# Latent attention scores: three products of 97 and 96 rows, or two full passes and one that two key tiles share

## The chip, the cores and the metric

The kernel runs as one program on one core of a Trainium2 chip. The metric is device time in microseconds (us) from the first to the last instruction of one execution; the time before is 2669.7 us, the median of 3 runs (2669.53 to 2672.55).

## The reference

One encoder layer is applied to two groups of tokens, 2048 of them ("sample", group 0) and 512 ("prompt", group 1), with shared weights and a model width of 1024. Every token is normalised, shifted and scaled, and projected; branch A is windowed attention, branch B is latent attention over all tokens of the group, and both are gated, merged and projected again. The change is in branch B's scores. It has 8 heads; a query and a key have 64 channels of their own (`nope`) and 32 rotary ones, and all heads share the rotary key:

```
q = concatenate([q_nope, q_rope]) * scale          # 96 channels
k = concatenate([k_nope, broadcast(k_rope)])       # 96 channels
s = einsum("bqhd,bkhd->bhqk", q_blk, k)
p = softmax(s);  o = einsum("bhqk,bkhd->bqhd", p, v)
```

## The kernel before, in words

Everything is computed to nearly float32 by splitting each operand into a high part, which the matmul takes in one pass, and a low part, the rest. A product is then high x high, low x high and high x low: three matmuls into one PSUM bank. Three stages follow one another. The first (lines 199 to 624) projects the tokens in five chunks of 512 (four of group 0, one of group 1) and writes queries, keys and values to DRAM. The second (lines 641 to 857) is latent attention. The third does the rest.

In the second stage a work item is one head and one chunk of 512 queries (`items`, line 772): per head four chunks of group 0 with 2048 keys each, and the one of group 1 with 512 keys. An item is cut into units of two key tiles of 128 keys, 8 units for group 0 and 2 for group 1: 34 units a head, 272 in all. The order of the engines' work in a unit is written out by hand (`SLOTS`, line 837, under a manual schedule):

- `load`: Q and, with a new head, K and V are fetched on the SP queue, in order (`q_load` 667, `load_k` 656, `load_v` 659, and `k_tile` 646, which fetches what all heads share once for each of the two K buffers).
- `s` (`s_mm`, 713): scores, transposed, keys x queries, two key tiles into two banks of one tile of PSUM, of which there are two. Each key tile takes three matmuls, over 97, 96 and 96 rows. Row 96 of K is all ones and row 96 of Q is minus the maximum of the query, so the scores come out with the maximum taken off.
- `row` (`row_mm`, 693): TensorE transposes an item's negated maxima into PSUM; ACT copies them (`row_copy`), to Q itself in the first items, later to DRAM, from where SP loads them into Q (`row_load`).
- `v` (`v_mm`, 752): two units later, the output: two matmuls of 128 x 128 weights with the exponentials' high part, two of 128 x 64 weights with the low part.
- `mp` and `red` (`mp_mm` 675, `mp_red` 684): ahead of an item, its maxima: the high x high product of 128 queries with 1024 keys into the only PSUM tile for it, and DVE's maximum over it. In the first two items this was done in the first stage.
- `exp`, `lo`, `sum`: ACT takes the exponential twice, once to the high type (`ph`) and once to float32 (`pf`); POOL subtracts them (`pl`); DVE adds `pf` to a running sum (line 748; at an item's first unit line 742, which adds two tiles of SBUF).
- `h`: from unit 220 on, the third stage's first activations are fetched, and from unit 230 split on ACT and DVE (line 638), with one weight tile after them (line 123).

Other matmuls that the prediction reads: lines 100 to 102 (`mm3`, the three products of a projection), line 561 (small float32 products at the start, whose 2-column weights stand in four column groups of the array), line 573 after them, and line 878 (the same kind in the third stage, among projections).

Of the kernel before, what the change touches and what calls it, by code (L numbers as in the profile page):

```python
# [10 lines left out]
F32R = mybir.dt.float32r  # L11
# [7 lines left out]
P = 128  # L19
D = 1024  # L20
KD = D // P
T = 512
# [11 lines left out]
def f(ap):  # L34
    return ap.bitcast(F32)
# [3 lines left out]
def encoder(ctx: ExitStack, tc: tile.TileContext, x_prompt, x_sample, c_prompt, c_sample, b_ada, g_norm, g_q,  # L39
            w_uq, g_kv, w_ukv, sink, g_final, t_mod, t_gate, t_col, t_a, t_b, t_oa, t_ob, t_out, rope_c, rope_s, bias, sel, y_prompt, y_sample):  # L40
    nc = tc.nc
# [36 lines left out]
    qn_d = [dram.tile([HB * 64, 2, T], F32, name=f"qn_d{c}") for c in range(NC)]  # L78
    qr_d = [dram.tile([HB * 32, 2, T], F32, name=f"qr_d{c}") for c in range(NC)]
    k_d = [dram.tile([HB, 64, 2, n * T], F32, name=f"k_d{n}") for n in (NS, 1)]  # L80
    kr_d = [dram.tile([32, 2, n * T], F32, name=f"kr_d{n}") for n in (NS, 1)]
# [8 lines left out]
    rw_d = [dram.tile([HB, 4, P], F32, name=f"rw_d{c}") for c in range(NC)]  # L90
    gate_d = dram.tile([2, D], F32, name="gate_d")
    ones_d = dram.tile([P, 1024], F32, name="ones_d")
# [115 lines left out]
    with psum("ps1a", 4) as pps["a"], psum("ps1t", 1) as pps["t"], psum("ps1c", 1) as pps["c"], \  # L208
# [307 lines left out]
        with pool("p0", "right") as p0:  # L516
# [36 lines left out]
            for q in range(4):  # L553
                pm = px(("t2", "t3")[q % 2], f"pm{q}")
                for k in range(0, KD, 2):
                    wa = p0.tile([P, 2, 2, 256], F32, name=f"wa{q}_{k}", tag="wa", bufs=WB)
                    nc.sync.dma_start(wa.rearrange("p i s n -> p (i s n)"), t_mod[q, k // 2])
                    for i in range(2):
                        for n in range(2):
                            r = 32 * (2 * i + n)  # L560
                            nc.tensor.matmul(pm[r:r + 2, 0:256], sc[:, k + i, :], wa[:, i, n, :], start=(k == 0),
                                             stop=(k == KD - 2))
                if q < 2:
                    pre.append(wload(p1a, f"a0_{2 * q}", r_loads(t_a, 512, 2 * q, 2), NR))
                for i in range(4):
                    r = 32 * i
# [8 lines left out]
                ks = slice(2 * q, 2 * q + 2)  # L575
# [65 lines left out]
    with psum("ps2s", 2) as pss, psum("ps2v", 1) as ps2v, psum("ps2", 1) as ps2, pool("p2k") as pk, pool("p2q") as pq, pool("p2a") as p2a, \  # L641
            pool("p2") as p2:
        NK = {0: 4 * NS, 1: 4}
        KT, VT = {0: [], 1: []}, {0: [], 1: []}

        def k_tile(g, i, tp):
            nk = NK[g]
            KT[g].append(tp.tile([97, 2, nk * P], F32R, name=f"K{g}_{i}"))
            nc.sync.dma_start(f(KT[g][i][96:97, 0, :]),
                              ones_d[0:nk // 8 or 1, 0:min(nk * P, 1024)].rearrange("(o a) b -> o (a b)", o=1))  # L650
            nc.sync.dma_start(f(KT[g][i][64:96]), kr_d[g])

        def v_tile(g, i, tp):
            VT[g].append(tp.tile([P, NK[g], P], F32R, name=f"V{g}_{i}"))

        def load_k(g, h):
            nc.sync.dma_start(f(KT[g][h % 2][0:64]), k_d[g][h])

        def load_v(g, h):
            nc.sync.dma_start(f(VT[g][h % 2]), v_d[g][h])  # L660
# [5 lines left out]

        def q_load(it):
            nm = it.nm
            it.Q = pq.tile([97, 2, T], F32R, name=f"Q{nm}", tag="Q", bufs=4)
            nc.sync.dma_start(f(it.Q[0:64]), qn_d[it.c][it.h * 64:(it.h + 1) * 64])  # L670
            nc.sync.dma_start(f(it.Q[64:96]), qr_d[it.c][it.h * 32:(it.h + 1) * 32])
            it.mx = pq.tile([P, 4, 2], F32, name=f"mx{nm}", tag="mx", bufs=5)
            it.ng = pq.tile([P, 4], F32, name=f"ng{nm}", tag="ng", bufs=5)

# [25 lines left out]

        def row_copy(it):
            if it in items[:ND]:
                nc.scalar.copy(it.Q[96:97, 0, :], it.rp[0:1, :])
                return
            rw = pq.tile([4, P], F32R, name=f"rw{it.nm}", tag="rw", bufs=2)
            nc.scalar.copy(rw, it.rp[0:4, 0:P])
            nc.sync.dma_start(rw_d[it.c][it.h], f(rw))
            row_load(it)

        def row_load(it):  # L710
            nc.sync.dma_start(f(it.Q[96:97, 0, :]), rw_d[it.c][it.h].rearrange("(o a) b -> o (a b)", o=1))

        def s_mm(it, p):
            K, Q, nm = KT[it.g][it.h % 2], it.Q, it.nm
            ps = pss.tile([P, 2, T], F32, name=f"s{nm}_{p}", tag="s")
            for j in range(2):
                ks = slice((2 * p + j) * P, (2 * p + j + 1) * P)
                nc.tensor.matmul(ps[:, j, :], K[0:97, 0, ks], Q[0:97, 0, :], start=True, stop=False)  # L718
                nc.tensor.matmul(ps[:, j, :], K[0:96, 1, ks], Q[0:96, 0, :], start=False, stop=False)  # L719
                nc.tensor.matmul(ps[:, j, :], K[0:96, 0, ks], Q[0:96, 1, :], start=False, stop=True)  # L720
            it.s = ps

        def s_exp(it, p, u):
# [52 lines left out]
        it = items[0]  # L776
        with tc.high_priority(offset=3000):
            k_tile(0, 0, pk)
            load_k(0, 0)
            q_load(it)  # L780
            row_load(it)
            v_tile(0, 0, p2a)
            load_v(0, 0)
            q_load(items[1])
            row_load(items[1])
# [10 lines left out]
        start = [sum(x.n for x in items[:n]) for n in range(len(items))]  # L796
# [14 lines left out]
        for n, it in enumerate(items):  # L811
            u0 = start[n]
            if n > 1:
                if it.c in (0, NS) and n in todo:
                    at(slot[n][0] - LQ - 2, "load", lambda it=it: (load_k(it.g, it.h), load_v(it.g, it.h)))
                u = max((slot[n][0] if n in todo else start[n]) - LQ, start[n - 3] if n > 3 else 0)
                at(u, "load", lambda it=it: q_load(it))
                if n not in todo:
                    at(u, "load", lambda it=it: row_load(it))
            if n in todo:  # L820
                for i in range(it.n):
                    x = "2" if (slot[n][i], "mp") in ev else ""
                    at(slot[n][i], "mp" + x, lambda it=it, i=i: mp_mm(it, i))
                    at(slot[n][i], "red" + x, lambda it=it, i=i: mp_red(it, i))
                at(slot[n][-1] + 1, "row", lambda it=it: row_mm(it))
                at(slot[n][-1] + 1, "rowc", lambda it=it: row_copy(it))
            for p in range(it.n):
                u = u0 + p
                at(u, "s", lambda it=it, p=p: s_mm(it, p))
                at(u, "exp", lambda it=it, p=p, u=u: s_exp(it, p, u))  # L830
                at(u, "lo", lambda it=it, p=p: s_lo(it, p))
                at(u, "sum", lambda it=it, p=p: s_sum(it, p))
                at(u + LA, "v", lambda it=it, p=p: v_mm(it, p))
            e = u0 + it.n
            at(e - 1 + LA, "oc", lambda it=it: o_copy(it))
# [7 lines left out]
        at(230 + 2 * KD, "h", lambda: W0.append(w_cols(p3r, "z0_1_0", C_ZB, NR, [(p3r, 1)], nc.vector)))  # L843
        neg = sorted({u for u, _ in ev if u < 0})
        k_tile(0, 1, p2a)
        v_tile(0, 1, p2a)
        for i in range(2):
            k_tile(1, i, p2)
            v_tile(1, i, p2)
# [9 lines left out]
    with psum("ps3a", 4) as pps["a"], psum("ps3t", 1) as pps["t"], psum("ps3c", 1) as pps["c"], pool("p3c") as p3c, pool("p3y") as p3y, pool("p3l") as p3, \  # L859
# [45 lines left out]
        for c in range(NC):  # L905
            g = 0 if c < NS else 1
# [66 lines left out]
            for j in range(KD):  # L973
# [3 lines left out]
                tp, tg = (p3, "M") if j else (p3y, "Y") if c + 1 < NC else (p3c, "r")  # L977
# [12 lines left out]
            for t in range(4):  # L990
                tp, tg = (p3y, "Y") if c + 1 < NC else (p3r, "H")
# [120 lines left out]
```

## Time and profile before

| | |
|---|---|
| median of 3 runs | 2669.7 us |
| the profiled execution | 2669.64 us |
| its span | 2666.4 us |
| TensorE busy | 97% of the span, 11842 matmuls |
| DVE, POOL, ACT busy | 64%, 62%, 50% |
| mean granted TensorE clock | 0.989 |
| second stage, first score to last | 529.6 to 1314 us |

The span is what the trace covers. A matmul's record is longer than the time by which the next one follows it, since they are pipelined; the distance of their starts is what one costs. PE is the matmuls and PEld the loads of their weights. "Idle before" of a group of instructions is how long its engine stood still ahead of them, with what ended it.

### The profile page before, as it was taken

How to read it: one execution, taken by the hardware profiler on the slowest of the kernel's cores; microseconds unless marked ns; L12 is line 12 of the kernel's file. 1: busy time of each engine (PE TensorE's matmuls, PEld its weight loads, DVE VectorE, ACT ScalarE, POOL GpSimd, SP SyncE). 2: the span in 40 equal slices, each digit the busy share in tenths (PEclk: the TensorE clock that was granted, in tenths of full speed). 3: DMA queues.
4: the chain of work that ended last, by engine and by line, in shares of the span. 5: the costliest groups of instructions: out<-in, count | busy, mean ns of one | idle time of the engine just before them, and what ended most of it. 6: DMA issues, size and time to landing. Idle time of an engine off the chain costs nothing. (4 is left out here: it accounts for less than half of the span.)

```text
span 2666.4 us, 33977 instructions
## 1 busy us (share of the span) xinstructions
PE 2579.6 (97%) x11842; PEld 2049.1 (77%) x11842; DVE 1698.3 (64%) x2507; ACT 1344.4 (50%) x2125; POOL 1649.8 (62%) x1012
## 2 busy tenths in 40 slices
PE   7999999899999999999999999999999999999998
PEld 4888888777777777776777778878887888778876
DVE  3664544589999999999665566446644663566325
ACT  3554533377777777776643444434444444443432
POOL 2564545288888888888852477346734773567345
PEclk9999999899999999999999999999999999999999
DMA  8677765553222322322264555444534453445341
GB/s 303 216 247 230 241 210 183 172 164 93 74 72 74 95 60 70 89 56 84 97 206 131 157 172 193 126 132 166 194 126 155 158 194 124 154 165 192 103 161 48
DMA packets 199431, 392.33 MB, mean 147 GB/s; under 512 B 18087, under 2 KB 97384, under 8 KB 197659
## 3 DMA queue, kind: packets, MB, share of 16 engines
q1 hardware_dynamic: 186210, 353.32, 41.6%
q10 hardware_dynamic: 13050, 36.86, 4.4%
q8 instruction: 93, 1.52, 0.2%
q14 instruction: 78, 0.63, 0.1%
HBM read 286.52 MB, written 103.58 MB: 146 GB/s over the span
## 5 line engine op out<-in xcount | busy, mean ns | idle before, releaser
L735 POOL TENSOR_TENSOR pl<-pf,ph 128x1024 fp32r<-128x1024 f32 x272 | 656.6, 2418 | 134.0 <-ACT pf L728 133.6
L123 POOL TENSOR_TENSOR wlgm<-wrgm,whgm 128x1024 fp32r<-128x1024 f32 x80 | 194.9, 2442 | 319.0 <-ACT whgm L122 261.0
L727 ACT ACTIVATE ph<-s 128x1024 fp32r<-128x1024 f32 x272 | 278.8, 1025 | 185.1 <-PE s L720 184.2
L686 DVE TENSOR_REDUCE mx<-mp 128x1 f32<-128x1024 f32 x240 | 292.7, 1220 | 38.7 <-PE mp L680 36.4
L748 DVE TENSOR_TENSOR ac<-ac,pf 128x512 f32<-128x512 f32 x424 | 294.2, 694 | 16.5 <-ACT pf L728 9.6
L728 ACT ACTIVATE pf<-s 128x1024 f32<-128x1024 f32 x272 | 275.7, 1014 | 0.0
L100 PE MATMUL gm<-H,whgm 128*128 128x512 f32 x640 | 251.7, 397 | 1.7 <-ACT whgm L122 1.7
L101 PE MATMUL gm<-H,wlgm 128*128 128x512 f32 x640 | 252.6, 395 | 0.0
L102 PE MATMUL gm<-H,whgm 128*128 128x512 f32 x640 | 251.4, 394 | 0.0
L718 PE MATMUL s<-Q,K 97*128 97x512 f32 x544 | 217.6, 400 | 3.2 <-DMA Q<-qr_d 3.2
L719 PE MATMUL s<-Q,K 96*128 96x512 f32 x544 | 217.6, 400 | 0.0
L720 PE MATMUL s<-Q,K 96*128 96x512 f32 x544 | 216.0, 397 | 0.0
L760 PE MATMUL a<-ph,V 128*128 128x512 f32 x544 | 175.1, 403 | 0.0
L763 PE MATMUL a<-pl,V 128*64 128x512 f32 x544 | 170.3, 394 | 1.0 <-POOL pl L735 0.8
L680 PE MATMUL mp<-K,Q 96*128 96x512 f32 x512 | 162.9, 399 | 6.7 <-DVE mx L686 5.0
L167 DVE CUSTOM_DVE_ANT_0 S<-as,mask,snk 128x384 f32<-128x384 f32 (+1 forms) x160 | 89.0, 587 | 98.9 <-PE as L165 75.5
L100 PEld LDWEIGHTS gm<-H,whgm 128*128 128x128 f32 x640 | 119.7, 188 | 26.8 <-ACT whgm L122 2.4
L102 PEld LDWEIGHTS gm<-H,whgm 128*128 128x128 f32 x640 | 120.7, 189 | 24.6
L101 PEld LDWEIGHTS gm<-H,wlgm 128*128 128x128 f32 x640 | 120.8, 189 | 23.9
L188 DVE TENSOR_TENSOR PT<-pT,PT 128x512 fp32r<-128x512 f32 x112 | 77.0, 687 | 96.3 <-ACT PT L187 95.4
L947 DVE SCALAR_TENSOR_TENSOR G<-G,po 128x512 f32<-128x512 f32 x80 | 53.5, 684 | 126.7 <-PE po L102 103.2
L102 PE MATMUL out<-wlw,M 128*128 128x512 f32 x320 | 124.3, 398 | 6.1 <-POOL wlw L123 6.0
(259 smaller groups left out, 6656.4 us busy)
## 6 DMA issues: line engine op xcount, KB each, us to landing
wrgm<-in_t_col_dram SPq DMA_DIRECT2D x80, 512.0 KB
wrz<-in_t_col_dram SPq DMA_DIRECT2D x40, 512.0 KB
wrw<-in_t_out_dram SPq DMA_DIRECT2D x40, 512.0 KB
wrqa<-in_t_col_dram ACTq DMA_DIRECT2D x20, 512.0 KB
qa_d<-qa SPq DMA_DIRECT2D x40, 256.0 KB
k_d<-kn SPq DMA_DIRECT2D x20, 512.0 KB
qn_d<-qn SPq DMA_DIRECT2D x20, 512.0 KB
v_d<-vt SPq DMA_DIRECT2D x20, 512.0 KB
```

Source lines behind the costliest of these rows:

```text
L100: nc.tensor.matmul(ps, wh, mh, start=first, stop=False)
L101: nc.tensor.matmul(ps, wl, mh, start=False, stop=False)
L102: nc.tensor.matmul(ps, wh, ml, start=False, stop=last)
L123: (eng or nc.gpsimd).tensor_tensor(out=wl[:, :n], in0=wr[:, :n], in1=f(wh[:, :n]), op=ALU.subtract)
L686: nc.vector.tensor_reduce(out=it.mx[:, i // 2, i % 2:i % 2 + 1], in_=it.mp.rearrange("p a b -> p (a b)"), axis=AX.X, op=ALU.max)
L718: nc.tensor.matmul(ps[:, j, :], K[0:97, 0, ks], Q[0:97, 0, :], start=True, stop=False)
L719: nc.tensor.matmul(ps[:, j, :], K[0:96, 1, ks], Q[0:96, 0, :], start=False, stop=False)
L720: nc.tensor.matmul(ps[:, j, :], K[0:96, 0, ks], Q[0:96, 1, :], start=False, stop=True)
L727: nc.scalar.activation(ph, it.s, AF.Exp)
L728: nc.scalar.activation(pf, it.s, AF.Exp)
L735: nc.gpsimd.tensor_tensor(out=pl, in0=it.pf[p], in1=f(it.ph[p]), op=ALU.subtract)
L748: nc.vector.tensor_tensor(out=sm if last and j else it.acc, in0=it.acc, in1=pf[:, j], op=ALU.add)
```

## The change

The 97 + 96 + 96 = 289 rows of a key tile's three products are laid out anew. K's tile gets 128 partitions. Its first half holds the high part of the key (64 + 32 rows) and the rotary high part once more (32); Q's first part holds the high part (96 rows) and the rotary low part (32). The second half of K holds the own channels' high and low parts (64 + 64), and meets Q's low and high ones. What is left, the rotary low part of the key with the high part of the query and the row of ones with the maxima (33 rows), goes into a third matmul. Its keys stand in a new tile `KC`, shared by the heads, in rows 0 to 32 for the even and rows 64 to 96 for the odd key tile of a unit, and the two third matmuls are issued one after the other behind the four full ones. Q's tile grows from two to three parts of 512 columns; the maxima go to rows 32 and 96 of the third part. The number of matmuls stays 6 a unit. The fetches change with the layout: Q in six transfers, not two, its maxima in two, not one, K in three, not one (1.5 MB, not 1 MB, for a head of group 0).

```diff
-            KT[g].append(tp.tile([97, 2, nk * P], F32R, name=f"K{g}_{i}"))
-            nc.sync.dma_start(f(KT[g][i][96:97, 0, :]), ones_d[...])
-            nc.sync.dma_start(f(KT[g][i][64:96]), kr_d[g])
+            KT[g].append(tp.tile([P, 2, nk * P], F32R, name=f"K{g}_{i}"))
+            for r in (64, 96):
+                nc.sync.dma_start(f(KT[g][i][r:r + 32, 0, :]), kr_d[g][:, 0, :])
+            if i == 0:
+                kc = tp.tile([97, nk // 2, P], F32R, name=f"KC{g}")
+                lo = kr_d[g][:, 1, :].rearrange("p (a s n) -> p s a n", s=2, n=P)
+                for s in range(2):
+                    nc.sync.dma_start(f(kc[64 * s:64 * s + 32]), lo[:, s])
+                    nc.sync.dma_start(f(kc[64 * s + 32:64 * s + 33]).rearrange("o a n -> o (a n)"),
+                                      ones_d[0:1, 0:nk // 2 * P])
+                KC[g] = kc
...
-            nc.sync.dma_start(f(KT[g][h % 2][0:64]), k_d[g][h])
+            K = KT[g][h % 2]
+            nc.sync.dma_start(f(K[0:64, 0, :]), k_d[g][h][:, 0, :])
+            nc.sync.dma_start(f(K[0:64, 1, :]), k_d[g][h][:, 0, :])
+            nc.sync.dma_start(f(K[64:128, 1, :]), k_d[g][h][:, 1, :])
...
-            it.Q = pq.tile([97, 2, T], F32R, name=f"Q{nm}", tag="Q", bufs=4)
-            nc.sync.dma_start(f(it.Q[0:64]), qn_d[it.c][it.h * 64:(it.h + 1) * 64])
-            nc.sync.dma_start(f(it.Q[64:96]), qr_d[it.c][it.h * 32:(it.h + 1) * 32])
+            it.Q = pq.tile([P, 3, T], F32R, name=f"Q{nm}", tag="Q", bufs=4)
+            qn, qr = qn_d[it.c][it.h * 64:(it.h + 1) * 64], qr_d[it.c][it.h * 32:(it.h + 1) * 32]
+            nc.sync.dma_start(f(it.Q[0:64, 0:2]), qn)
+            nc.sync.dma_start(f(it.Q[64:128, 1]), qn[:, 0])
+            nc.sync.dma_start(f(it.Q[64:96, 0]), qr[:, 0])
+            nc.sync.dma_start(f(it.Q[96:128, 0]), qr[:, 1])
+            for r in (0, 64):
+                nc.sync.dma_start(f(it.Q[r:r + 32, 2]), qr[:, 0])
...
-                nc.scalar.copy(it.Q[96:97, 0, :], it.rp[0:1, :])
+                nc.scalar.copy(it.Q[32:33, 2, :], it.rp[0:1, :])
+                nc.scalar.copy(it.Q[96:97, 2, :], it.rp[0:1, :])
...
-            nc.sync.dma_start(f(it.Q[96:97, 0, :]), rw_d[it.c][it.h].rearrange("(o a) b -> o (a b)", o=1))
+            for r in (32, 96):
+                nc.sync.dma_start(f(it.Q[r:r + 1, 2, :]), rw_d[it.c][it.h].rearrange("(o a) b -> o (a b)", o=1))
...
-                nc.tensor.matmul(ps[:, j, :], K[0:97, 0, ks], Q[0:97, 0, :], start=True, stop=False)
-                nc.tensor.matmul(ps[:, j, :], K[0:96, 1, ks], Q[0:96, 0, :], start=False, stop=False)
-                nc.tensor.matmul(ps[:, j, :], K[0:96, 0, ks], Q[0:96, 1, :], start=False, stop=True)
+                nc.tensor.matmul(ps[:, j, :], K[:, 0, ks], Q[:, 0, :], start=True, stop=False)
+                nc.tensor.matmul(ps[:, j, :], K[:, 1, ks], Q[:, 1, :], start=False, stop=False)
+            for j in range(2):
+                r = slice(64 * j, 64 * j + 33)
+                nc.tensor.matmul(ps[:, j, :], KC[it.g][r, p, :], Q[r, 2, :], start=False, stop=True)
```

## Rows read from the trace of the kernel before

**Rows 1.** By stretch: us, busy of PE, PEld, DVE, ACT, POOL, clock, DMA share, GB/s.
```profile
600.00:700.00 100.00, 99.21 (x426) 74.29 (x425) 93.45 (x103) 71.74 (x82) 83.27 (x35) 1.00 0.30 86
1200.00:1300.00 100.00, 95.32 (x389) 69.97 (x389) 90.70 (x105) 70.41 (x82) 82.70 (x34) 0.97 0.22 67
```

**Rows 2.** Timeline of TensorE, a unit in mid-stage: start, length, line, operation.
```profile
808.85 0.40 PE L718 MATMUL s<-Q,K 97*128 97x512 f32 x1
...
810.25 0.62 PE L760 MATMUL a<-ph,V 128*128 128x512 f32 x2
810.71 0.63 PE L763 MATMUL a<-pl,V 128*64 128x512 f32 x2
811.17 0.63 PE L680 MATMUL mp<-K,Q 96*128 96x512 f32 x2
811.64 0.40 PE L718 MATMUL s<-Q,K 97*128 97x512 f32 x1
```

**Rows 3.** Timeline of DVE over an item's first unit and the next two.
```profile
803.40 1.23 DVE L686 TENSOR_REDUCE mx<-mp 128x1 f32<-128x1024 f32 x1 [0.23 <-PE mp L680]
804.54 2.56 DVE L742 TENSOR_TENSOR ac<-pf 128x512 f32<-128x512 f32 x1
807.02 1.21 DVE L686 TENSOR_REDUCE mx<-mp 128x1 f32<-128x1024 f32 x1
808.15 1.42 DVE L748 TENSOR_TENSOR ac<-ac,pf 128x512 f32<-128x512 f32 x2
809.48 1.22 DVE L686 TENSOR_REDUCE mx<-mp 128x1 f32<-128x1024 f32 x1
```

**Rows 4.** Timeline of TensorE: the transposes of the maxima, one item apart.
```profile
621.59 0.27 PE L699 MATMUL mt<-ident,ng 128*4 128x128 f32 x1 [0.20 <-DVE ng L691]
...
644.46 0.27 PE L699 MATMUL mt<-ident,ng 128*4 128x128 f32 x1 [0.20 <-DVE ng L691]
```

**Rows 5.** Timeline of POOL at the stage's first and last units.
```profile
534.54 14.67 POOL L735 TENSOR_TENSOR pl<-pf,ph 128x1024 fp32r<-128x1024 f32 x6 [10.63 <-ACT pf L728]
551.24 2.40 POOL L735 TENSOR_TENSOR pl<-pf,ph 128x1024 fp32r<-128x1024 f32 x1 [2.03 <-ACT pf L728]
...
1293.09 26.47 POOL L735 TENSOR_TENSOR pl<-pf,ph 128x1024 fp32r<-128x1024 f32 x11 [0.95 <-ACT pf L728]
```

**Rows 6.** Timeline of TensorE: four column groups at once, early in the kernel.
```profile
21.23 0.62 PE L561 MATMUL pm<-wa,cols 128*2 128x256 f32 x8
21.77 0.61 PE L573 MATMUL pc<-fold,mod 98*128 98x4 f32 x4
```

**Rows 7.** Timeline of TensorE: column groups of 2 between full passes.
```profile
1365.67 0.39 PE L102 MATMUL po<-Y,who 128*128 128x512 f32 x1
1365.99 1.03 PE L878 MATMUL pg<-wrg,cols 128*2 128x512 f32 x4
1366.95 0.50 PE L100 MATMUL po<-Y,who 128*128 128x512 f32 x1
```

**Rows 8.** Timeline of the weight loads there.
```profile
1365.99 0.10 PEld L878 LDWEIGHTS pg<-wrg,cols 128*2 128x2 f32 x4 [0.35 <-issue]
1366.94 0.19 PEld L100 LDWEIGHTS po<-Y,who 128*128 128x128 f32 x1 [0.86 <-ACT G L961]
1367.05 0.19 PEld L164 LDWEIGHTS as<-KA,QA 128*128 128x128 f32 x1
```

**Rows 9.** Timeline of SP's issues (start, length) before the second stage.
```profile
516.09 0.46 SPq L649 DMA_DIRECT2D K<-ones_d  x1
...
520.20 0.58 SPq L671 DMA_DIRECT2D Q<-qr_d  x1
```

**Rows 10.** Timeline of TensorE: the stage's first score matmul and its wait.
```profile
529.59 0.77 PE L718 MATMUL s<-Q,K 97*128 97x512 f32 x1 [3.21 <-DMA Q<-qr_d]
```

**Rows 11.** Busy time by stretch around the stage's start (columns as in rows 1).
```profile
525.00:530.00 5.00, 1.79 (x12) 1.45 (x11) 2.52 (x4) 1.66 (x3) 0.00 (x0) 0.92 0.94 216
530.00:535.00 5.00, 5.00 (x13) 3.79 (x13) 0.50 (x1) 1.94 (x2) 0.46 (x1) 0.50 1.04 407
```

More of the change, by code (lines that the diff above doesn't have):

```diff
@@ L643, in encoder @@
         NK = {0: 4 * NS, 1: 4}
-        KT, VT = {0: [], 1: []}, {0: [], 1: []}
+        KT, VT, KC = {0: [], 1: []}, {0: [], 1: []}, {}
         def k_tile(g, i, tp):
             nk = NK[g]
-            KT[g].append(tp.tile([97, 2, nk * P], F32R, name=f"K{g}_{i}"))
-            nc.sync.dma_start(f(KT[g][i][96:97, 0, :]),
-                              ones_d[0:nk // 8 or 1, 0:min(nk * P, 1024)].rearrange("(o a) b -> o (a b)", o=1))
-            nc.sync.dma_start(f(KT[g][i][64:96]), kr_d[g])
+            KT[g].append(tp.tile([P, 2, nk * P], F32R, name=f"K{g}_{i}"))
[9 more added lines that the diff above has]
+                KC[g] = kc
         def v_tile(g, i, tp):
```

## The prediction

> **What bounds the kernel now.** I read the page's shares first: TensorE is busy for 97% of the span, far ahead of every other engine. Shares over the span hide stages, so the next view is busy time by stretch. In the middle of the second stage [rows 1] TensorE works 99.2 of 100 us, but DVE stands at 93.5 and POOL at 83.3: TensorE sets the pace and DVE follows 6% behind it. From unit 230 on (1200 to 1300 us) TensorE falls to 95.3 with DVE at 90.7: there other work mixes in. Then the timeline of TensorE, for the price of one matmul: from one unit's first score to the next one's lie 12 matmuls in 811.64 - 808.85 = 2.79 us, 0.2325 us each, whatever their rows (96, 97 or 128) or weight columns (64 or 128) [rows 2]. An item of eight such units takes 644.46 - 621.59 = 22.87 us, which is 8 x 2.79 = 22.32 and 0.55 for its transpose of the maxima and the waits around it [rows 4]. At the stage's ends it is POOL: its subtractions run back to back, 16.70 us for the first 7 units (2.39 each) and 26.47 for the last 11 (2.41 each), since these units have no maxima to compute and TensorE's ten matmuls would need only 2.33 [rows 5].
>
> **The change part by part.** The sum is made against the profiled execution, 2669.64 us (span 2666.4 and some 3 us around it); the median of the runs, 2669.7, is the same.
>
> *The score matmuls.* Six remain in a unit, but the last two use rows 0 to 63 and 64 to 127 of the array and write different banks. If they run at once, a unit has 11 slots, 2.56 us instead of 2.79, and an item saves 8 x 0.2325 = 1.86 us. No row of this trace shows two halves of the rows at work together. The nearest shows it for columns: eight matmuls of 256 columns in four column groups take 21.77 - 21.23 = 0.54 us, where one by one, at half of 0.2325, they would take 0.93 [rows 6]. One slot is the least, since each still streams 512 columns. On the dear side stand three things. The second half's weights: a load that nothing hides takes 1367.05 - 1366.94 = 0.11 us [rows 8], so two take 0.22, just under the slot of the matmul ahead; if the second one is not fetched that early, the pair costs 0.11 more. The change of the array's shape into the pair and out of it: going from 128 to 64 weight columns and back costs nothing now (starts at 810.25, 810.71, 811.17: 0.46 for each two) [rows 2]; but where 2-column weights in column groups stand between full passes, the array is free at 1365.67 + 0.23 = 1365.90, the group starts at 1365.99, and the next full weights are loaded only when it is through, 0.11 in the open [rows 7, 8]. That makes 0.09 + 0.11, with the pair's own load 0.31 a unit at worst. Last, no sharing at all: 0.23. So the extra is between 0 and 0.31 a unit; I take 0, from rows 2, because these are the same kind of matmul in the same stage.
>
> *What the saving meets.* Two waits give part of it back in each item. First, the transpose of the maxima already waits for DVE, 0.20 us in both rows [rows 4]: it follows the scores, which now end one slot sooner, while the maximum that it needs does not. That unit gains nothing: -0.23. Second, DVE. An ordinary unit costs it 809.48 - 807.02 = 2.46 us, under the new 2.56; but an item's first unit costs 807.02 - 803.40 = 3.62, because its sum of two tiles takes 2.48 [rows 3]. The next maximum comes 3.62 - 2.56 = 1.06 late, and there is only one PSUM tile for maxima: TensorE's next pair of maxima must wait for it. Its slack is the nine matmuls between two pairs (2.09) less 0.2 until DVE starts and 1.23 for the maximum: 0.66. So 0.4 of stall, less what DVE's idle just before absorbs (0.23 [rows 3]): between 0.2 and 0.4, I take 0.3. An item gains 1.86 - 0.23 - 0.30 = 1.33 us. DVE's own sum is a floor: 3.62 + 7 x 2.46 = 20.84, under the new 22.87 - 1.33 = 21.54.
>
> Of the 272 units, 7 at the start and 11 at the end go at POOL's pace and gain nothing; if POOL's cover were gone they would gain 0.23 each. The 31 from unit 230 on have DVE and ACT busy with the next stage's activations as well, and TensorE idles 4.7 us already [rows 1]: between 0 and 5 us, I take 1. The 223 others are 27.9 items' worth: 37.1 us.
>
> *The fetches.* For the first item SP issues 6 transfers from 516.09 on, the last one right behind 520.20 [rows 9], and TensorE then stands 3.21 us until Q is there [rows 10], with the DMA engines at 0.94 to 1.04 of their time [rows 11]. So whatever is added lies on the path. The change makes 17 transfers of these 6 (the shared rotary part 2 + 4 in place of 2, K 3 in place of 1, Q 6 in place of 2, the maxima 2 in place of 1) and 1.0 MB more: 0.5 for K, 0.25 each for Q and for the rotary rows. 11 issues at about 0.5 us are 5.5 us; 1.0 MB at the 407 and 216 GB/s of these stretches are 2.5 and 4.7 us. These overlap: 2.5 to 5.5, I take 5. The clock is no further loss: it is granted at half, 1.2 GHz, in 530 to 535 already, after the wait [rows 11]. The loads for the second K buffer and the next Qs follow at full DMA as well, with 0.9 MB more, partly under POOL's pace: 0 to 9, I take 2. Together +7 (2 to 14). Later in the stage the DMA engines are at 0.30 [rows 1], and five issues more per item (2.5 us of SP's time in 21.5) are hidden; behind them in SP's queue stand the stores of sums and outputs, which nobody awaits, and the maxima's way into Q, due three units (7.7 us) later. ACT's second copy of the maxima is in three items only, under 1 us. If that cover were gone, see the fifth case.
>
> Sum: 2669.6 - 37.1 - 1 + 7 = 2638.5, so 2639 us.
>
> **The rivals.**
> 1. *As forecast*: 2639, by the bounds above (stalls 0.2 to 0.4, fetches 2 to 14, the late units 0 to 5) 2625 to 2655.
> 2. *The second half's weights come late*, 0.11 a unit. An item then gains 1.86 - 0.88 - 0.23 = 0.75 (a slower unit has no stall from DVE), 21 in all: 2669.6 - 21 - 1 + 7 = 2655. For it: in rows 2's kind of stream a weight load starts with the matmul before its own, and only one stands ahead. Against it: the four loads of rows 8 start together within 0.1 us.
> 3. *The change of shape costs time at both ends, slower than before.* Place: the entry into the pair and the first matmul behind it, in each unit. It decides from 0.23 a unit, where it eats the slot. With rows 7 and 8 as its price, 0.31, a unit is 0.08 longer: 254 x 0.08 = 20, and 7 for the fetches: 2697; with 0.20 (the pair's own load hidden) the gain is about 7 in 28 items and goes to the fetches: 2670. For it: rows 7 and 8; against it: rows 2, where a change of column shape is free. The Trainium skill states in TensorEngine Tiling (Array Packing), Key Properties, that changing the tiling mode, and not only the tile, drains TensorE; by that rule this case would be the result. The trace agrees with it in rows 7 and 8 (0.09 and 0.11 us) and not in rows 2 (no gap).
> 4. *The change doesn't do what it says*: the halves run one after the other. Six slots remain and the fetches are added: 2677. Against it only rows 6, which are columns, not rows.
> 5. *Fetches too late all through the stage*: the start costs 14, and SP, which issues in order and waits there for free Q tiles, brings the maxima 1 us too late to some 29 items: 2669.6 - 38 + 14 + 29 = 2675, and between that and 2639 if fewer. Against it: three units' margin.
>
> **How the numbers follow.** Chances: 0.53 for the first, 0.14, 0.15, 0.08 and 0.10 for the others. The time is that of the first, 2639. The range goes from 2622 (no stall and the cheapest start) up through cases 2, 4 and 5 and most of case 3, to 2690. A measurement of this kernel tells 0.2%, 5.3 us, from no change. Faster than 2664.3: nearly all of 1 and 2 and half of 5, 0.71; within it: the low end of 3 and parts of 4 and 5, 0.09; slower: 0.20.
>
> **What would show it.** Right: the two 33-row matmuls of a unit start within some 20 ns of each other, the next matmul 0.23 behind, and 808.85 to 811.64 becomes 2.56; two transposes eight units apart stand 21.5 us apart; DVE is busy 96 to 97% in mid-stage and TensorE shows new waits for the maximum (line 686's successor), once an item; the wait before the first score is about 8 us. Wrong: a gap of 0.1 or more before or behind the pair (3), the second start 0.11 behind the first (2) or 0.23 behind (4), or score matmuls that wait for a transfer to Q in mid-stage (5). A DVE that paces every unit would leave less than 1.3 us an item without any gap at the pair.

## The result and the profile after

The changed kernel takes 2711.68 us (median of 4 runs, 2703.72 to 2716.47) against 2671.12 for the kernel before (4 runs): a ratio of 1.0148, 95% interval 1.0129 to 1.0167. It is slower by 40 us (1.5%), clear of noise, where 32 us less was forecast (2639 against 2671); 2711.68 lies outside the range of 2622 to 2690. The profiled execution took 2708.36 us with a span of 2706.6, 40.2 more than before's.

The page's totals hardly differ from before's; TensorE is again busy for 97% of the span. The stretches of the second stage show more (columns as in [rows 1]):

```profile
600.00:700.00 100.00, 98.70 (x409) 63.01 (x408) 88.58 (x100) 68.41 (x78) 79.82 (x34) 1.00 0.34 94
1200.00:1300.00 100.00, 94.19 (x368) 58.46 (x367) 92.14 (x98) 69.47 (x82) 79.93 (x33) 0.95 0.33 97
```

In the first of them TensorE is as busy as before with 409 matmuls in 100 us, not 426, and all the engines that follow it do less: DVE 88.6, not 93.5. So DVE doesn't pace the stage; TensorE does, at a slower pace. Its busy time doesn't tell that: 409 slots of 0.2325 us are 95 us, and the records cover 98.7. The timeline of one unit, which answers to [rows 2], shows where (start, length, line, operation):

```profile
902.69 0.39 PE L735 MATMUL s<-Q,K 128*128 128x512 f32 x1
...
903.15 0.39 PE L735 MATMUL s<-Q,K 128*128 128x512 f32 x1
903.39 0.40 PE L736 MATMUL s<-Q,K 128*128 128x512 f32 x1
903.71 0.49 PE L739 MATMUL s<-Q,KC 33*128 33x512 f32 x2
904.14 0.72 PE L779 MATMUL a<-ph,V 128*128 128x512 f32 x2
904.70 0.62 PE L782 MATMUL a<-pl,V 128*64 128x512 f32 x2
905.16 0.62 PE L695 MATMUL mp<-K,Q 96*128 96x512 f32 x2
905.63 0.39 PE L735 MATMUL s<-Q,K 128*128 128x512 f32 x1
```

And its weight loads:

```profile
903.16 0.19 PEld L736 LDWEIGHTS s<-Q,K 128*128 128x128 f32 x1
903.71 0.19 PEld L739 LDWEIGHTS s<-Q,KC 33*128 33x128 f32 x2 [0.37 <-issue]
904.14 0.30 PEld L779 LDWEIGHTS a<-ph,V 128*128 128x128 f32 x2 [0.24 <-ACT o L787]
```

The two 33-row matmuls do share the array: two records, together 0.49 us long, which is the length of one, with both loads in 0.19. But the last full matmul before them starts at 903.39 and is through after its 0.2325 us, at 903.62; the pair's loads begin at 903.71, not under it, as the load at 903.16 does under the matmul that starts at 903.15. Behind the pair it is the same: the next full weights are loaded at 904.14, when the pair is done, and so the first of the two L779 costs a load more. (The trace names ACT there; it is not the cause, since in 165 other units the same gap stands with nothing that was waited for.) From the last full matmul's start to L782's lie 904.70 - 903.39 = 1.31 us for four slots (0.93): the visit to half-row matmuls costs 0.38 us. It saves one slot of 0.2325. A unit takes 905.63 - 902.69 = 2.94 us, not 2.79. The list of waits has the entry for all 272 units and the exit for 165; in the others another instruction stands behind the pair, or another releaser is named (waiter, releaser: us in total, times, longest):

```profile
PEld s L739 <- issue: 101.8, 272, 0.7
PEld a L779 <- issue: 41.2, 165, 0.4
```

"issue" means that nothing in the profile was waited for. Against [rows 4], the transposes of the maxima stand 23.88 us apart, not 22.87 (view: timeline of TensorE):

```profile
716.44 0.27 PE L714 MATMUL mt<-ident,ng 128*4 128x128 f32 x1 [0.24 <-DVE ng L706]
...
740.32 0.27 PE L714 MATMUL mt<-ident,ng 128*4 128x128 f32 x1 [0.24 <-DVE ng L706]
```

Eight units lose 8 x (0.38 - 0.23) = 1.2, and the transpose's wait gives 0.2 back. The first score answers to [rows 10], with a wait of 7.7 us, not 3.2:

```profile
530.79 0.76 PE L735 MATMUL s<-Q,K 128*128 128x512 f32 x1 [7.68 <-DMA Q<-rw_d]
```

The start of each unit's first score, from the timelines, locates the rest (us; full97 and split_dma are the experiments below):

```
unit    before    changed          full97          split_dma
0       529.6     530.8  + 1.2     532.2  + 2.6    536.4  + 6.8
8       553.1     565.7  +12.7     561.9  + 8.8    567.3  +14.3
34      628.7     646.5  +17.9     639.1  +10.5    642.9  +14.2
229     1186.9    1227.7 +40.9     1197.4 +10.6    1201.0 +14.2
271     1313.1    1360.3 +47.2     1320.8 + 7.8    1328.7 +15.6
```

In the 195 units from 34 to 229 the changed kernel loses 23.0 us. It loses 17.9 up to unit 34, and in the 42 last ones 6.3. The third stage then takes 7 us less than before's; why stays open. Each column is one execution. How far two executions of the same fetches differ is seen from col32, which has before's layout and transfers: its starts stand 0.0 from before's at unit 34, 0.5 at unit 229 and 2.0 at unit 271.

At the two ends the granted clock of TensorE is part of the difference. In the changed kernel TensorE waits 4.7 us for a Q in unit 5, and the clock then stands at its lower level, 1.2 GHz (0.50), until about 566; before's trace has 1.00 there. The units 6 and 7 take 5.29 us each, in full97 4.09 and 2.78 (timeline of TensorE; then by stretch, the changed kernel and before, the clock third from the end):

```profile
554.15 1.19 PE L695 MATMUL mp<-K,Q 96*128 96x512 f32 x2 [4.74 <-DMA Q<-qr_d]
555.14 0.63 PE L735 MATMUL s<-Q,K 128*128 128x512 f32 x1
...
560.43 0.63 PE L735 MATMUL s<-Q,K 128*128 128x512 f32 x1
```

```profile
560.00:565.00 5.00, 5.00 (x13) 3.01 (x12) 2.53 (x3) 1.83 (x2) 2.31 (x1) 0.50 1.05 228
560.00:565.00 5.00, 5.00 (x23) 3.75 (x22) 4.93 (x7) 3.77 (x4) 4.42 (x2) 1.00 1.03 329
```

In the last 42 units it is 0.97 before, 0.95 in the changed kernel and 1.00 in full97, with waits for the maxima of 4.4 to 5.0 us in each (in this order):

```profile
1186.90:1313.10 126.20, 119.11 (x491) 87.38 (x490) 115.27 (x124) 91.32 (x106) 107.06 (x45) 0.97 0.26 77
1227.70:1360.30 132.60, 126.39 (x491) 78.06 (x490) 111.17 (x124) 91.37 (x106) 107.59 (x45) 0.95 0.25 75
1197.40:1320.80 123.40, 116.03 (x490) 84.97 (x489) 110.00 (x124) 91.45 (x106) 107.06 (x45) 1.00 0.28 83
```

With one trace of each kernel it is not shown whether these stretches of low clock belong to the kernel or to the execution.

### The profile page after: what moved, and what is told of

It reads as the page before. It is cut to its first block, busy times and chain, and to the rows that moved or that the text cites. A ratio compares the mean times of both kernels' runs of the same rounds, so it can differ in the third digit from the quotient of the medians.

```text
span 2706.6 us, 34262 instructions
## 1 busy us (share of the span) xinstructions
PE 2615.1 (97%) x11842; PEld 1986.9 (73%) x11842; DVE 1689.7 (62%) x2507; ACT 1347.9 (50%) x2128; POOL 1647.3 (61%) x1012
## 5 line engine op out<-in xcount | busy, mean ns | idle before, releaser
L735 PE MATMUL s<-Q,K 128*128 128x512 f32 x544 | 219.4, 403 | 7.7 <-DMA Q<-rw_d 7.7
L736 PE MATMUL s<-Q,K 128*128 128x512 f32 x544 | 218.9, 402 | 0.0
L779 PE MATMUL a<-ph,V 128*128 128x512 f32 x544 | 195.9, 441 | 0.2 <-ACT o L787 0.2
L782 PE MATMUL a<-pl,V 128*64 128x512 f32 x544 | 174.5, 402 | 0.6 <-POOL pl L754 0.6
L739 PE MATMUL s<-Q,KC 33*128 33x512 f32 x544 | 138.0, 504 | 0.0
L695 PEld LDWEIGHTS mp<-K,Q 96*128 96x128 f32 x512 | 97.4, 192 | 47.7 <-DVE mx L701 6.3
```

The lines of the kernel that those rows point to most:

```text
L695: nc.tensor.matmul(ps[:, j, :], Q[0:96, 0, qt * P:(qt + 1) * P], K[0:96, 0, kc * T:(kc + 1) * T], start=True, stop=True)
L735: nc.tensor.matmul(ps[:, j, :], K[:, 0, ks], Q[:, 0, :], start=True, stop=False)
L736: nc.tensor.matmul(ps[:, j, :], K[:, 1, ks], Q[:, 1, :], start=False, stop=False)
L779: nc.tensor.matmul(it.a, V[:, 2 * p + j, :], it.ph[p][:, j, :], start=(p == 0 and j == 0), stop=last and j == 1)
```

## The experiments

The theory (S): going to half-row matmuls and back costs a fixed time a visit, more than the slot that the sharing saves. Rivals: the transfers slow mid-stage (L); the two matmuls slow each other (C).

**full97.** The third matmul reads 97 rows, with zeros for the other key tile in `KC`, which becomes twice as large; the rest of the layout and the transfers stay, with one transfer more for each Q.

```diff
...
-                r = slice(64 * j, 64 * j + 33)
-                nc.tensor.matmul(ps[:, j, :], KC[it.g][r, p, :], Q[r, 2, :], start=False, stop=True)
+                nc.tensor.matmul(ps[:, j, :], KC[it.g][0:97, j, p, :], Q[0:97, 2, :], start=False, stop=True)
```

> The changed kernel with its layout and transfers, but the third matmul of a key tile reads 97 rows (zeros in the half that is not its own), so no matmul of the stage uses half of the rows; one more transfer per Q, and 4 KB a partition more. Theory S (going to half-row matmuls and back costs a fixed 0.4 us a visit, and gives back one slot of 0.23): mid-stage units fall from 2.98 us to the old 2.86, heads in mid-stage take 97.4 us; the loss of the stage's first 34 units, some 17 us against before, stays, since it comes from the transfers; time 2680 to 2690 us. Rival L (the mid-stage loss comes from the transfers, 0.12 a unit): units stay at 2.98, time some 2710. Rival C (the two matmuls at once slow each other by sharing PSUM or SBUF): units fall as in S, so only the next runs tell it from S.

Measured: 2674.66 us (10 runs) against 2673.07 (13 runs), ratio 1.0005, interval 0.999 to 1.002.

```profile
902.44 0.40 PE L736 MATMUL s<-Q,K 128*128 128x512 f32 x1
...
903.37 0.63 PE L739 MATMUL s<-Q,KC 97*128 97x512 f32 x2
903.84 0.62 PE L779 MATMUL a<-ph,V 128*128 128x512 f32 x2
...
905.22 0.40 PE L736 MATMUL s<-Q,K 128*128 128x512 f32 x1
```

The gaps are gone and a unit is back at 2.78. From unit 34 to 229 nothing is lost against before, with even more bytes than the change: L falls. The transfers do cost, but only at the stage's start: 10.5 us by unit 34. I had expected 17, the changed kernel's loss, in which visits and the low clock are contained; so the time came out under the 2680 to 2690 expected. At the stage's end it is 7.8, the granted clock being 1.00 in the last units. The time against before, 1.6 us more, is not clear of none. Against this kernel the half-row pair costs the changed one 2711.7 - 2674.7 = 37 us, or 39 if each is taken against the runs of before beside it.

**same_half.** The third matmuls of both key tiles use rows 0 to 32, one after the other; `KC` is laid out to match.

```diff
...
-                r = slice(64 * j, 64 * j + 33)
-                nc.tensor.matmul(ps[:, j, :], KC[it.g][r, p, :], Q[r, 2, :], start=False, stop=True)
+                nc.tensor.matmul(ps[:, j, :], KC[it.g][0:33, j, p, :], Q[0:33, 2, :], start=False, stop=True)
```

> The changed kernel, but the third matmuls of both key tiles use rows 0 to 32, one after the other, so nothing is shared, while the visit to half-row matmuls stays. S: the stretch from the last full score matmul's start to the next full matmul's second start grows by one slot, 0.21 to 0.23, units in mid-stage 3.2 us, time about 2711 + 255 x 0.23 = 2768. C: each of the two, alone, costs 0.11 to 0.2 less than in the pair, so the unit grows by 0.1 or less, under 2735.

Measured: 2761.62 us (one run).

```profile
899.85 0.40 PE L736 MATMUL s<-Q,K 128*128 128x512 f32 x1
900.18 0.73 PE L738 MATMUL s<-Q,KC 33*128 33x512 f32 x2
900.84 0.74 PE L778 MATMUL a<-ph,V 128*128 128x512 f32 x2
901.41 0.62 PE L781 MATMUL a<-pl,V 128*64 128x512 f32 x2
...
902.33 0.40 PE L735 MATMUL s<-Q,K 128*128 128x512 f32 x1
...
905.50 0.40 PE L735 MATMUL s<-Q,K 128*128 128x512 f32 x1
```

A unit takes 3.17, 0.23 more than with the pair shared: sharing is worth its whole slot, and C falls. From 899.85 to 901.41 lie 1.56 us for five slots (1.16): the visit costs 0.40, with nothing shared.

**one_visit** and **two_visits.** The kernel before, its layout and transfers, with the third product cut to 64 rows (the rotary part of high x low is left out). In one_visit both stand behind the four others; in two_visits each stays where it was, and its edit is this:

```diff
-                nc.tensor.matmul(ps[:, j, :], K[0:96, 0, ks], Q[0:96, 1, :], start=False, stop=True)
+                nc.tensor.matmul(ps[:, j, :], K[0:64, 0, ks], Q[0:64, 1, :], start=False, stop=True)
```

> The kernel before, its layout and transfers, with only the third product of each key tile cut to 64 rows (the rotary part of high x low is left out) and both third products put behind the four others: six slots, one visit to half-row matmuls a unit, nothing shared. S: the first score of a unit to that of the next 2.79 + 0.4 = 3.2 us, stage longer by 255 x 0.4 = 102, time about 2773. L and C: 2.79, time 2671.

> As one_visit, but each third product stays behind its own two, so the array goes to half-row matmuls and back twice a unit. S: 2.79 + 0.8 = 3.6 us a unit, time about 2671 + 255 x 0.8 = 2875. If the price hangs on each half-row matmul, not on each visit, it equals one_visit. L and C: 2671.

Measured: 2756.32 and 2865.36 us (one run each). The timeline of one_visit:

```profile
900.97 0.40 PE L718 MATMUL s<-Q,K 97*128 97x512 f32 x1
...
902.00 0.73 PE L722 MATMUL s<-Q,K 64*128 64x512 f32 x2
902.65 0.73 PE L762 MATMUL a<-ph,V 128*128 128x512 f32 x2
...
904.14 0.40 PE L718 MATMUL s<-Q,K 97*128 97x512 f32 x1
```

And of two_visits:

```profile
901.77 0.40 PE L718 MATMUL s<-Q,K 97*128 97x512 f32 x1
902.00 0.39 PE L719 MATMUL s<-Q,K 96*128 96x512 f32 x1
902.33 0.50 PE L720 MATMUL s<-Q,K 64*128 64x512 f32 x1
902.75 0.50 PE L718 MATMUL s<-Q,K 97*128 97x512 f32 x1
...
905.34 0.40 PE L718 MATMUL s<-Q,K 97*128 97x512 f32 x1
```

Units of 3.17 and 3.57 against 2.79: 0.38 for one visit, 0.78 for two. With the same twelve slots, nothing of the change's layout and the same number of half-row matmuls, the price goes with the visits. The times, one run each, came 10 to 17 us under the expected ones; I had counted 255 units at 0.4, and the ones with a transpose gain part of it back, which need not be all of it.

**col32.** The prediction had taken its zero from a change in the columns [rows 2]. Here the low part of the output has 32 weight columns instead of 64 (half of its channels' low part is left out).

```diff
-                        nc.tensor.matmul(it.a[0:64, :], V[:, 2 * p + j, 64:128], it.pl[p][:, j, :], start=False,
+                        nc.tensor.matmul(it.a[0:32, :], V[:, 2 * p + j, 64:96], it.pl[p][:, j, :], start=False,
```

> The kernel before, with the low part of the output cut from 64 to 32 weight columns (half of its channels' low part is left out): the only change of shape left in the stage is then 128 to 32 columns and back, instead of 128 to 64. S in its wide form (every change of the array's shape costs 0.4 us, and 64 columns were an exception): a unit goes from 2.79 to about 3.2 us, time about 2770. S in its narrow form (only a change in the rows costs): 2.79 us, time 2671.

Measured: 2670.92 us (one run). There is no gap on either side of line 763:

```profile
902.06 0.40 PE L720 MATMUL s<-Q,K 96*128 96x512 f32 x1
902.30 0.63 PE L763 MATMUL a<-pl,V 128*32 128x512 f32 x2
902.77 0.62 PE L760 MATMUL a<-ph,V 128*128 128x512 f32 x2
```

So rows 2 were read rightly and don't bear on the question: in this stage the number of weight columns changes freely, the step to half of the rows doesn't.

**two_per_visit.** The full matmuls of two units, then the half-row ones of both.

```diff
...
+            if p % 2:
+                return
+            it.s = {}
+            for i in (p, p + 1):
+                ps = it.s[i] = pss.tile([P, 2, T], F32, name=f"s{nm}_{i}", tag="s")
...
+            for i in (p, p + 1):
+                for j in range(2):
+                    r = slice(64 * j, 64 * j + 33)
+                    nc.tensor.matmul(it.s[i][:, j, :], KC[it.g][r, i, :], Q[r, 2, :], start=False, stop=True)
```

> The changed kernel, but the eight full matmuls of two units come first, then the four half-row ones of both in one visit. If the price is one of the visit (S), TensorE's own work for two units is 22 slots x 0.2325 + 0.39 = 5.5 us; but both score tiles of PSUM are then taken together, and after the visit ACT needs 2.1 us for the first unit's two exponentials and 4.0 for both before the second tile is free, then come 0.93 of full matmuls, 0.2 of entry and 0.43 of half-row ones: 5.75 us for two units, 2.88 a unit with transposes 2.9 to 2.95; time 2680 to 2700, between the two kernels. If the price is one of each half-row pair, 2.98 a unit or more and 2711 or more. In neither case does it beat the kernel before.

Measured: 2795.06 us (4 runs), ratio to before 1.0458, interval 1.0441 to 1.0476. That is far above the 2680 to 2700 of S. The other case, with 2711 or more, had no upper end, so the time alone would speak for it; the timeline decides.

```profile
906.17 0.40 PE L740 MATMUL s<-Q,K 128*128 128x512 f32 x1
906.50 0.73 PE L744 MATMUL s<-Q,KC 33*128 33x512 f32 x4
907.16 0.72 PE L783 MATMUL a<-ph,V 128*128 128x512 f32 x2
907.72 0.63 PE L786 MATMUL a<-pl,V 128*64 128x512 f32 x2
```

The visit itself does what S says: 907.72 - 906.17 = 1.55 for five slots (1.16), 0.39 with four matmuls in it as with two. What I had missed is the maxima (waits in 600 to 1200 us):

```profile
PEld mp L695 <- DVE mx L701: 56.2, 66, 0.9
...
PE mt L714 <- DVE ng L706: 32.1, 20, 1.6
...
PE mp L695 <- DVE mx L701: 25.9, 66, 0.4
```

With the second unit's scores moved ahead, only four matmuls (0.93 us) stand between two pairs of maxima, which share one PSUM tile that DVE holds for 1.4 us (0.2 until it starts, 1.2 for the maximum); and after them comes a long stretch without any.

**full97_act.** full97, with the shared rows and ones of the other three K tiles fetched from ACT's queue.

```diff
...
+            q = nc.sync if (g, i) == (0, 0) else nc.scalar
             for r in (64, 96):
-                nc.sync.dma_start(f(KT[g][i][r:r + 32, 0, :]), kr_d[g][:, 0, :])
+                q.dma_start(f(KT[g][i][r:r + 32, 0, :]), kr_d[g][:, 0, :])
...
```

> full97 (which lost 10 us against before over the stage's first 26 units, and nothing later), with the shared rotary rows and ones of the other three K tiles fetched from ACT's queue, not SP's. If the loss is SP's issue time, one transfer behind the other, the loss by unit 26 falls from 10.5 to 5 us or less, and the wait of the maxima for Q (3.4 us near 554 us) goes. If it is the DMA engines' time for the added bytes, it stays within 2 us of 10.

Measured: 2698.66 us (one run). It answers nothing of what it asked: the exponentials stood behind these transfers in ACT's queue, 30.3 us at once (waits of 526 to 640 us):

```profile
ACT ph L747 <- DMA KC<-kr_d: 30.3, 1, 30.3
```

**split_dma.** The kernel before, its layout, matmuls and bytes, in 16 transfers instead of 6 before the first score: Q in six, as shown, and K in three, the shared rotary rows in four and the maxima in two.

```diff
...
-            nc.sync.dma_start(f(it.Q[0:64]), qn_d[it.c][it.h * 64:(it.h + 1) * 64])
-            nc.sync.dma_start(f(it.Q[64:96]), qr_d[it.c][it.h * 32:(it.h + 1) * 32])
+            for r in (0, 32):
+                nc.sync.dma_start(f(it.Q[r:r + 32]), qn_d[it.c][it.h * 64 + r:it.h * 64 + r + 32])
+            for r in (0, 8, 16, 24):
+                nc.sync.dma_start(f(it.Q[64 + r:72 + r]), qr_d[it.c][it.h * 32 + r:it.h * 32 + r + 8])
...
```

> The kernel before, its layout, matmuls and bytes, but cut into as many transfers as the change has: Q in six and its maxima in two, K in three, the shared rotary rows in four; 16 transfers instead of 6 before the first score. If the 10 us that full97 loses in the stage's first 26 units are SP's issue time (some 0.5 us a transfer), this kernel loses 5 us or more there, by unit 26 against before. If they are the DMA engines' time for the added 1.0 to 2 MB, it loses under 2 us.

Measured: 2685.89 us (one run, beside 2673.27 for one of before); 14.2 us are lost by unit 34, none later until unit 229. The stretch before the first score:

```profile
520.00:525.00 5.00, 4.36 (x24) 3.48 (x22) 2.67 (x5) 2.44 (x5) 1.90 (x5) 1.00 0.60 88
525.00:530.00 5.00, 0.00 (x0) 0.00 (x0) 1.24 (x2) 0.41 (x1) 0.00 (x0) 0.92 0.64 102
530.00:535.00 5.00, 0.00 (x0) 0.00 (x0) 0.00 (x0) 0.00 (x0) 0.00 (x0) 0.50 0.44 102
```

Without one byte more, the number (and the smaller size) of the transfers alone delays the stage by more than full97's do (10.5), with the DMA engines at 0.44 to 0.64 of their time. In the changed kernel and in full97 they stood at 1.00 to 1.05 from 520 to 530 and at 0.74 to 0.85 from 530 to 535, so there the added bytes may count as well; the two shares were not separated.

## Why the prediction was wrong

*The step that failed* is "So the extra is between 0 and 0.31 a unit; I take 0, from rows 2, because these are the same kind of matmul in the same stage." The extra is 0.38 a unit, above even the dear end. Two things were wrong in it. The row taken for the nearest was not: a change in columns was taken for a change in rows, and col32 shows that columns are free at 32 as at 64. And the dear end, from [rows 7, 8], had a gap only on entry (0.09) and a load at each end. Here the entry has a gap of 903.71 - 903.62 = 0.09 and an open load of 0.11; if the pair streams for one slot behind that, it is through at 904.05, and the exit has 904.14 - 904.05 = 0.09 and a load again. These four pieces make 0.40, where 0.38 to 0.40 is measured as a sum; the term that the dear end lacked is the gap behind the pair. The rule that the prediction set beside its third rival, the Trainium skill's in TensorEngine Tiling (Array Packing), Key Properties, that a change of the tiling mode drains TensorE, agrees with what the half-row matmuls cost here (0.38 to 0.40 us a visit in five kernels). Whether 64 or 32 weight columns are a change of mode by that rule, no run shows; they have no gap (col32).

*The third rival was right in its place and in the point from which it decides* (0.23 a unit), at a price of 0.38 instead of 0.31; it gave 2697, for 2711.7 measured, and had a chance of 0.15 against 0.53 for the forecast.

*Sharing* was right: one slot, both starts together, both loads at once (rival 2 falls), worth 0.23 (same_half; rival 4 falls).

*What the saving meets*: the transpose of the maxima does wait as before, 0.24 us, and so an item gives back 0.2 of the loss instead of losing part of a gain. The stall behind an item's first unit, 0.30, didn't arise, since the unit grew; as a price it is untested.

*The fetches*, +7 (2 to 14): full97 shows 10.5 us in the stage by unit 34 and 7.8 at its end; in the time it is 1.6 us, within its interval of none. The wait ahead of the first score, forecast at about 8 us, is 7.7, but that is luck: the score starts only 1.2 us later than before, since TensorE came to it 3.3 us earlier (523.1, not 526.4), and most of the loss comes behind it, by unit 8. There the prediction's "The clock is no further loss" fails, with the units 6 and 7 at 1.2 GHz. POOL's pace at the start was misread as well: the first line of [rows 5] has six subtractions in 14.67 us, 2.45 each, and then a wait of 2.03, not seven in 16.70 back to back. SP's issues did not delay anything in mid-stage (rival 5 falls).

*The sum*: with 8 x (0.38 - 0.23) - 0.23 = +0.97 an item for -1.33, the same 27.9 items give +27, and with the fetches 2669.6 + 27 + 7 = 2704. The missing 8 us are not accounted for one by one. The changed kernel loses 7.4 more than full97 in the first 34 units, of which the visits explain some 4 and the lower clock of the units 6 and 7 some 3 (3.7 more than full97's, less their two visits), and 6.3 against before in the last 42, which I had taken for covered; the third stage takes 7 less.

## What to carry to other kernels

Half-row matmuls that share the array save one slot for each pair, and a visit to them among full-row matmuls costs 0.4 us here, 1.7 slots of 512 columns: by that it would pay from the second pair in a visit on (0.46 saved, 0.39 paid), not with one, if nothing else is moved for it. That is an estimate: the one kernel here with two pairs in a visit lost more by what was moved, and none became faster. Count visits, not matmuls. And where the trace lacks an operation, ask in what the row at hand differs from it (here rows against columns) before its zero is taken, and work out the price at which the forecast turns.

## What the runs showed of the hardware that was not expected

- A change from matmuls of 96 and more rows to ones of 33 or 64 rows and back costs 0.38 to 0.40 us, whether the visit holds one, two or four matmuls; a change from 128 to 64 or 32 weight columns costs nothing in the same stream ([rows 2], col32). The traces show the gap and the open load at each end, not their reason. Where between 64 and 96 rows the price begins, and why [rows 7, 8], with 2 columns in column groups and plain float32 operands, show gaps, was not tried.
- Two weight loads for different halves of the rows run at the same time (both within 0.19 us in the changed kernel, against 0.29 to 0.30 for two on one half in same_half).
- The same fetches cut into 16 transfers instead of 6 put the first score 6.8 us later and unit 34 14.2 us later (split_dma, one run), with the DMA engines at 0.44 to 0.64.
